# A gate's column sums: from dot products on VectorE to scaled rows added up in DRAM

## The chip, the core and the metric

The kernel runs on one core of one Trainium2 chip. The metric is the device time of one execution in microseconds (us), as the median over the runs. TensorE is called PE here, VectorE DVE, ScalarE ACT, GpSimd POOL; SP is the engine that issues most transfers.

## The reference, cut to what matters

The reference is one decoder block on 512 tokens of width 1024, with a conditioning vector `c`. All that the change touches hangs on the first line:

```
mod = silu(c) @ w_ada + b_ada                                  # 1024 x 6144
shift1, scale1, gate1, shift2, scale2, gate2 = split(mod, 6)
h = rms_norm(x, norm1_g) * (1.0 + scale1) + shift1
z = h @ w_in            # u, v (gMLP), q, k, v, indexer q, k, weights, branch gates g_a, g_b
...                     # gMLP gives y_a; sparse attention (indexer, top 256 keys, softmax) gives y_b
merged = sigmoid(g_a) * (y_a @ w_proj_a) + sigmoid(g_b) * (y_b @ w_proj_b)
x = x + gate1 * (merged @ w_out)
h2 = rms_norm(x, norm2_g) * (1.0 + scale2) + shift2
x = x + gate2 * ((silu(f_g) * f_u) @ w_ffn_out)                # f_g, f_u = split(h2 @ w_ffn_in)
```

`mod` is a product of a vector with a matrix of 24 MB: six sections of 1024 outputs, each a sum over 1024 channels. In the attention, each query keeps the 256 best keys by an indexer score, which here means 16 rounds of "take the eight largest, strike them out" for a block of 128 queries with enough keys.

## The kernel before, in words

**The matrix products.** PE works in float32 by three products of rounded parts: every weight chunk is split into a rounded part `hi` (ACT, line 167) and a remainder `lo` (DVE or POOL, line 171), and each product is hi*hi + hi*lo + lo*hi (`mm3`, lines 105 to 109). A chunk is 128 x 1024 elements, 512 KB.

**The stream.** The weights come in one list `stream`, written by hand in the order of use. Between the weight chunks stand the rows of `w_ada` ("m" entries). `get(i)` returns chunk `i` and first calls `ensure`, which splits all chunks up to two ahead and does the work of every row that lies between; `room` says how many loads may be under way. Weight chunks share a ring of three `raw` tiles. Rows have tiles of their own (`mraw`) up to the end of the branch projections, use the `raw` ring in the stretch of the branch gates `W_GB`, and other tiles after that.

**The rows.** For section `s` and outputs 128*kt to 128*kt + 127, `mod_row(s, kt)` loads a tile of 128 outputs by 1024 channels and forms 128 dot products with silu(c), which stands in all partitions of `csb`. It does so in one of two ways: by one DVE instruction that multiplies and sums (line 270), or, with `pool=True`, by a product on POOL (line 266) and a summing copy on ACT (line 267). The latter is deferred through `part_sum` and `flush_rows`, by two calls of `get`. Section 4 is gate1, 2 and 3 are shift2 and scale2. The generator `mods_mid` gives the rows their order: eight of gate1, eight of section 2 (from the third on with POOL), eight of section 3. Gate1 is needed along the free axis; so after its last row `gate_out` turns it (a transpose on DVE, four writes to DRAM) and `gate_in` reads it back into all partitions, both called from a list of due times (`sec_done`, counted by `tick`).

**The order around the change.** After the gMLP products come eight groups, two weight chunks each: ga(0), ga(1), pa(0), pa(1), ga(2), pa(2), ga(3), pa(3), so 16 chunk steps, 0 to 15 (`au_tasks`, line 1280). In each step DVE is given some of the top-k work: `run_bg` takes from a list as much as a budget in us says (`BG`, line 1272, with 3.9 for steps that it doesn't name). In steps 12 and 13, after that, the first queries are split (`at_split`, line 1297). In steps 14 and 15 attention starts, and from then on `at_step(s)` (line 1482) runs the attention units, a block of 128 queries and two heads each, in a pipeline: scores on PE (`at_qk`), mask and maximum on DVE (`at_soft_a`), exponential on ACT (`at_exp`), normalisation on DVE (`at_soft_b`), turning, and the product with the values (`at_pv`). The first four units are turned through DRAM: DVE transposes (`at_turn`), SP writes (`at_out`), POOL reads back (`at_in`, tile `ld`), and `at_halves` splits. Between them, `gb_part` gives PE pieces of the branch gate B (tiles `pgb`, copied by ACT to `gb`, line 1477). Steps 2 to 7 take up to 2 us of top-k each (line 1514), and `need_sco` (line 893) forces what is left when a unit needs its mask: units 0 to 3 the mask of query block 3, units 4 to 7 block 2, units 8 to 11 block 1.

**Queues.** Each engine does its instructions in the order in which the code emits them, and an instruction that waits holds up all behind it. SP issues the loads; POOL issues the adding transfers and the reads of `ld`.

Of the kernel before, what the change touches and what calls it, by code (L numbers as in the profile page):

```python
# [58 lines left out]
def block_kernel(ctx: ExitStack, tc: tile.TileContext, x, x_t, w_in,  # L59
# [67 lines left out]
    def issue(i):  # L127
        e = stream[i]
        if e["kind"] == "m" and e["early"]:
            k = mrot[0]  # L130
            mrot[0] += 1
            raw = s2pair(k % 8, F32).rearrange("p a n -> p (a n)")
        elif i in last_raw:
            raw = last_raw[i]()
        elif e["kind"] == "m" and e["mid"]:
            k = e["mid"]
            if k == "A2":
                k = ("G1", "A2")[mrot[1] % 2]
                mrot[1] += 1
            raw = mid.tile([128, 1024], F32, name="mraw", tag=k, bufs=1)  # L140
        else:
            raw = base.tile([128, 1024], F32, name="raw", tag="raw", bufs=RAWB)
        e["raw"] = raw
        if e["kind"] == "m":
            e["dma"](raw)
            return
        k0, nk, n = e["kts"][0], len(e["kts"]), e["n"]
        e["view"] = lambda t: t[:, :nk * n].rearrange("p (j n) -> p j n", j=nk)
        SY.dma_start(raw[:, :nk * n], e["src"](k0, nk, e["c0"] if isinstance(e["c0"], tuple) else ((e["c0"], n),)))
        if i in W1[2:7]:  # L150
            load_xt(W1.index(i) + 1)
# [37 lines left out]
    def room(i):  # L189
        e = stream[i]  # L190
        if i in last_raw:
            return True
        pend = [stream[k] for k in range(st["prep"], i) if k not in last_raw]
        if e["kind"] == "m" and e["early"]:
            return sum(p["kind"] == "m" for p in pend) < 8
        if e["kind"] == "m" and e["mid"]:
            return all(p["kind"] == "w" for p in pend) and len(pend) <= 1
        return sum(p["kind"] == "w" or not (p["early"] or p["mid"]) for p in pend) + len(part_sum) < RAWB


    def get(i, ahead=2):
        k = wseq.index(i)
        asked[0] += 1
        flush_rows(2)
        ensure(wseq[min(k + ahead, len(wseq) - 1)])
        return chunk[i]

# [9 lines left out]
    mid = mid_stack.enter_context(tc.tile_pool(name="mid", bufs=1))  # L217
    csb = base.tile([128, D], F32, name="csb", tag="csb", bufs=1)
    crow = mid.tile([128, D], F32, name="crow", tag="A0", bufs=1)[0:1]
    pack = mid.tile([128, 211], F32, name="pack", tag="A2", bufs=1)  # L220
    SY.dma_start(pack, small)
    A.dma_start(crow, c_row)
    vmid = mid_stack.enter_context(tc.tile_pool(name="vmid", bufs=1))
# [15 lines left out]
    dram = ctx.enter_context(tc.tile_pool(name="dram", bufs=1, space=bass.MemoryType.DRAM))  # L239
    grow = [dram.tile([1, D], F32, name=f"grow{g}") for g in range(2)]  # L240

    part_sum, asked = [], [0]

    def flush_rows(age):
        while part_sum and part_sum[0][0] + age <= asked[0]:
            part_sum.pop(0)[1]()

    def mod_row(s, kt, pool=False):
        k = slice(kt, kt + 1)
        if s < 4:  # L250
            o = G1[:, s, k] if s < 2 else Gc[:, 1, 8 * (3 - s) + kt:8 * (3 - s) + kt + 1]
        else:
            o = gcol[:, 8 * (s - 4) + kt:8 * (s - 4) + kt + 1]
        scale, init = ((1.0, bsh1), (n1c[:, k], bsc1), (1.0, bsh2), (n2c[:, k], bsc2), (1.0, bg1), (1.0, bg2))[s]

        whole = s > 1 or kt
        parts = [slice(0, D)] if whole else [slice(0, 512), slice(512, D)]
        sums = [init[:, k], o] if whole else [init[:, k], half_sum[:, s:s + 1], o]

        def dma(raw):  # L260
            for c in list(parts):
                SY.dma_start(raw[:, c], w_shsc[s * D + kt * 128:s * D + (kt + 1) * 128, c])

        def fn(raw, n=2):
            if pool:
                P.tensor_mul(raw, raw, csb)
                part_sum.append((asked[0], lambda: A.activation(raw, raw, AF.Copy, scale=scale, accum_out=o)))
                return
            for c in [parts.pop(0) for _ in range(min(n, len(parts)))]:
                V.tensor_tensor_reduce(out=raw[:, c], in0=raw[:, c], in1=(csb if s > 1 else pc)[:, c], scale=scale,  # L270
                                       scalar=sums.pop(0), op0=OP.mult, op1=OP.add, accum_out=sums[0])
        return dma, fn

    def gate_out(g):
        V.transpose(gturn, gcol)
        rows = grow[g].rearrange("o (k b j) -> (o k) b j", b=4, j=32)
        for b in range(4):
            SY.dma_start(rows[:, b], gturn[32 * b + 8 * g:32 * b + 8 * g + 8])

    def gate_in(g):  # L280
        SY.dma_start(gate_b[1 + g], grow[g][0].partition_broadcast(128))

    def gate1_row(kt):
        dma, dot = mod_row(4, kt)

        def fn(raw):
            dot(raw)
            if kt == 7:
                sec_done.append((tick[0] + 2, lambda: gate_out(0)))
                sec_done.append((tick[0] + 5, lambda: gate_in(0)))  # L290
        return dma, fn

    def group(src, c0, n=256, K=8, mods=None, pool=False, where=None, nm=1, mraw="A2"):
        ids = []
# [18 lines left out]
    W_Q += [group(w_in, 2048 + 256 * g) for g in range(2, 4)]  # L313

    def mods_mid():
        for kt in range(8):
            yield gate1_row(kt)
        for s in (2, 3):
            for kt in range(8):
                yield mod_row(s, kt, s == 2 and kt > 1)  # L320
    mm_ = mods_mid()
    W_GA, W_PA = {}, {}
    for kind, g in (("a", 0), ("a", 1), ("p", 0), ("p", 1), ("a", 2), ("p", 2), ("a", 3), ("p", 3)):
        if kind == "a":
            W_GA[g] = group(w_in, 4168 + 256 * g, pool=2 * (g > 1), mods=mm_ if g > 1 else None)
        else:
            W_PA[g] = group(w_pa, 256 * g, pool=2, mods=mm_ if g < 3 else None)
    W_GB = [group(w_in, 5192 + 256 * g, pool=2 * (g == 1), mods=mm_ if g else None, mraw=False) for g in range(4)]
    for i in W_GB[1]:
        stream[i]["lo"] = V  # L330
# [96 lines left out]
    V.tensor_copy(cols[:, 0:67], pack[:, 0:67])  # L427
    posi = pack[:, 67:195].bitcast(I32)
    P.tensor_copy(half_sum[:, 16:32], pack[:, 195:211])
    lng, lnb, wrow = half_sum[:, 16:24], half_sum[:, 24:32], gcol[:, 16:24]  # L430

    ones = mid.tile([128, 128], F32, name="ones", tag="A3", bufs=1)
# [836 lines left out]
    austep = [0, 0]  # L1269
    MM = {0: [3, 4], 1: [5, 6], 2: [7]}  # L1270
    EV = {0: [1, 2], 1: [3, 4], 2: [5, 6], 3: [7]}
    BG = {0: 0.0, 1: 0.0, 2: 0.0, 3: 1.0, 4: 1.8, 5: 2.5, 7: 2.5, 8: 1.8, 11: 2.5, 12: 3.0, 13: 3.0, 14: 1.0, 15: 1.0}
    PT = {4: [pq0.turn], 5: [pq0.put], 6: [pq0.scatter, pq4.fetch], 8: [pq4.turn], 9: [pq4.put], 10: [pq4.scatter]}

    def au_post():
# [4 lines left out]
    def au_tasks():  # L1280
        s = austep[0]
        austep[0] += 1
        if s == 0:
            k_b(1)
        for m in EV.get(s, []):
            mix_ev(m)
        for fn in PT.get(s, []):
            fn()
        run_bg(BG.get(s, 3.9))
        if s in (12, 13):  # L1290
            at_split(s - 12)

    aun = [(i, hp) for i in (3, 2, 1, 0) for hp in range(4)]
    AS = {}
# [252 lines left out]
    for s in range(2, NU + 3):  # L1547
        at_step(s)

    flush_rows(0)  # L1550
    V.tensor_add(Gc[:, 1, 10:16], Gc[:, 1, 10:16], bsh2[:, 2:8])
    for g in range(4):
        A.activation(gbt[g], gbt[g], AF.Sigmoid)
    for i in range(4):
# [796 lines left out]
```

## Time and profile before

| | |
|---|---|
| median of the 3 runs | 809.16 us (807.22 to 810.09) |
| the profiled execution's own time | 807.56 us |
| its span | 805.8 us |
| mean granted clock of TensorE | 0.985 |
| instructions | 13081 |
| row loads of `w_ada` into `mraw`, into `raw` | 26 of 512 KB, 6 of 512 KB |

The span runs from the first to the last instruction of the profiled execution; 1.8 us lie around it. In the timeline a line holds the start in us, the duration in us, engine, line of the kernel, operation, result <- operands, shapes and count; the bracket at its end is the idle time of that engine ahead of it and what ended it. In the tables of stretches each engine's column is its busy time in us, with the number of instructions behind it.

### The profile page before, as it was taken

How to read it: one execution, taken by the hardware profiler on the slowest of the kernel's cores; microseconds unless marked ns; L12 is line 12 of the kernel's file. 1: busy time of each engine (PE TensorE's matmuls, PEld its weight loads, DVE VectorE, ACT ScalarE, POOL GpSimd, SP SyncE). 2: the span in 40 equal slices, each digit the busy share in tenths (PEclk: the TensorE clock that was granted, in tenths of full speed). 3: DMA queues.
4: the chain of work that ended last, by engine and by line, in shares of the span. 5: the costliest groups of instructions: out<-in, count | busy, mean ns of one | idle time of the engine just before them, and what ended most of it. 6: DMA issues, size and time to landing. Idle time of an engine off the chain costs nothing.

```text
span 805.8 us, 13081 instructions
## 1 busy us (share of the span) xinstructions
PE 778.0 (97%) x4867; PEld 701.7 (87%) x4867; DVE 692.7 (86%) x1115; ACT 464.1 (58%) x829; POOL 192.0 (24%) x266
## 2 busy tenths in 40 slices
PE   8999999999999998799999999999999999999996
PEld 6899899999888786678887789999999999888885
DVE  7979778878899989987669888989999888898886
ACT  6665567575512356456625577556565656766654
POOL 5981323220244214312020010312122222100001
PEclk9999999999999998999999999999999999999999
DMA  9965777784476467227692612689987977566672
GB/s 356 414 183 165 172 177 198 192 239 142 131 235 198 143 165 203 79 74 236 238 274 66 204 58 79 176 256 290 259 287 201 281 197 210 162 193 197 217 226 108
DMA packets 56610, 158.71 MB, mean 197 GB/s; under 512 B 15873, under 2 KB 16513, under 8 KB 56546
## 3 DMA queue, kind: packets, MB, share of 16 engines
q1 hardware_dynamic: 43152, 118.49, 43.7%
q0 software_dynamic: 12816, 38.43, 20.4%
q8 instruction: 38, 0.62, 0.3%
q10 hardware_dynamic: 578, 0.95, 0.3%
q14 instruction: 26, 0.21, 0.1%
HBM read 151.53 MB, written 28.72 MB: 224 GB/s over the span
## 4 chain that ended last, share of the span: by engine, by line
PE 66%; DVE 19%; ACT 5%; DMA 4%; issue 4%; POOL 1%; SPq 0%; POOLq 0%; DVEq 0%; ACTq 0%
PE R L107 8%; PE R L109 8%; PE R L108 8%; PE pfo L109 4%; PE pfo L108 4%; PE pfo L107 4%; PE pav L107 3%; PE pav L108 3%; PE pav L109 3%; DVE mraw L270 3%; DMA mraw<-in_w_shsc_dram 2%; DVE sco L874 2%; PE pb L107 2%; PE pb L109 2%; PE pb L108 2%
## 5 line engine op out<-in xcount | busy, mean ns | idle before, releaser
L167 ACT ACTIVATE hi<-raw 128x1024 fp32r<-128x1024 f32 (+4 forms) x90 | 90.4, 1007 | 80.3 <-PE pfo L109 22.6
L171 DVE TENSOR_TENSOR lo<-raw,hi 128x1024 fp32r<-128x1024 f32 (+3 forms) x70 | 84.6, 1209 | 23.3 <-ACT hi L167 23.2
L108 PE MATMUL pfo<-lo,za 128*128 128x512 f32 (+1 forms) x144 | 55.2, 383 | 0.0
L109 PE MATMUL pfo<-hi,za 128*128 128x512 f32 (+1 forms) x144 | 55.2, 383 | 0.0
L107 PE MATMUL pfo<-hi,za 128*128 128x512 f32 (+1 forms) x144 | 55.2, 383 | 0.0
L401 POOL COPY sm<-sm 128x1 f32<-128x1 f32 x36 | 24.0, 666 | 103.4 <-ACT sm L400 103.3
L107 PE MATMUL pb<-h,hi 128*128 128x512 f32 (+1 forms) x128 | 48.5, 379 | 0.0
L109 PE MATMUL pb<-h,lo 128*128 128x512 f32 (+1 forms) x128 | 48.1, 376 | 0.0
L108 PE MATMUL pb<-h,hi 128*128 128x512 f32 (+1 forms) x128 | 48.1, 376 | 0.0
L270 DVE CUSTOM_DVE_ANT_0 mraw<-mraw,csb,cols 128x1024 f32<-128x1024 f32 x26 | 38.2, 1471 | 7.2 <-DMA mraw<-in_w_shsc_dram 7.2
L171 POOL TENSOR_TENSOR lo<-raw,hi 128x1024 fp32r<-128x1024 f32 x12 | 29.1, 2428 | 63.6 <-ACT hi L167 63.6
L107 PE MATMUL R<-tb,sx 128*128 128x256 f32 x160 | 44.2, 276 | 0.0
L109 PE MATMUL R<-tb,sx 128*128 128x256 f32 x160 | 44.2, 276 | 0.0
L108 PE MATMUL R<-tb,sx 128*128 128x256 f32 x160 | 44.2, 276 | 0.0
L107 PE MATMUL R<-tb,hi 128*128 128x256 f32 x160 | 44.2, 276 | 0.0
L108 PE MATMUL R<-tb,hi 128*128 128x256 f32 x160 | 44.2, 276 | 0.0
L109 PE MATMUL R<-tb,lo 128*128 128x256 f32 x160 | 44.2, 276 | 0.0
L381 POOL DMA_DIRECT2D wsum<-in_w_ffn_out_dram x24 | 19.6, 831 | 62.5 <-DMA wsum<-wsum 35.4
L108 PEld LDWEIGHTS pfo<-lo,za 128*128 128x128 f32 x144 | 27.1, 188 | 5.4
L107 PEld LDWEIGHTS pfo<-hi,za 128*128 128x128 f32 x144 | 27.1, 188 | 5.3
L109 PEld LDWEIGHTS pfo<-hi,za 128*128 128x128 f32 x144 | 27.1, 188 | 5.3
L107 PE MATMUL pgb<-h,hi 128*128 128x512 f32 x64 | 27.8, 434 | 3.9 <-ACT gb L1477 3.9
(438 smaller groups left out, 2908.4 us busy)
## 6 DMA issues: line engine op xcount, KB each, us to landing
raw<-in_w_ffn_in_dram SPq DMA_DIRECT2D x44, 512.0 KB, 5.6
raw<-in_w_in_dram SPq DMA_DIRECT2D x36, 512.0 KB, 3.6
wsum<-in_w_ffn_out_dram POOLq DMA_DIRECT2D x30, 512.0 KB, 7.3
mraw<-in_w_shsc_dram SPq DMA_DIRECT2D x26, 512.0 KB, 4.1
raw<-wsum SPq DMA_DIRECT2D x20, 512.0 KB, 4.1
s<-in_w_shsc_dram SPq DMA_DIRECT2D x14, 512.0 KB, 8.1
raw<-in_w_ffn_out_dram SPq DMA_DIRECT2D x13, 512.0 KB, 3.9
wsum<-wsum POOLq DMA_DIRECT2D x10, 512.0 KB, 5.7
```

Source lines behind the costliest of these rows:

```text
L107: T.matmul(o, wh, rh, start=start, stop=False, **kw)
L108: T.matmul(o, wh, rlo, start=False, stop=False, **kw)
L109: T.matmul(o, wlo, rh, start=False, stop=stop, **kw)
L167: A.activation(hi[:, :m], e["raw"][:, :m], AF.Copy)
L171: e["lo"].tensor_sub(lo[:, :m], e["raw"][:, :m], f(hi[:, :m]))
L270: V.tensor_tensor_reduce(out=raw[:, c], in0=raw[:, c], in1=(csb if s > 1 else pc)[:, c], scale=scale, scalar=sums.pop(0), op0=OP.mult, op1 ...
L381: P.dma_start(wsum_at(n, c), src, max_dma_last_dim=4096, accum_op=OP.add)
L401: P.tensor_copy(t, t)
L874: V.match_replace(out=sco[i], in_to_replace=m8s[i], in_values=sco[i], imm_value=TAKEN)
```

## The change

Gate1 is no longer formed by dot products. Its part of `w_ada` is handed over untransposed, so that a row tile holds 128 channels by 1024 outputs. ACT scales each tile by silu(c) of its channels (one factor for each partition, `ccol`); POOL writes the first scaled tile to `gacc` in DRAM and adds the other seven to it by adding transfers. What is left to sum are the 128 partitions: two adding transfers within DRAM fold 128 rows to 64 and to 32, four loads bring these into SBUF in blocks of 32 by 32, DVE transposes and sums them and adds the bias. Then `gate_out` and `gate_in` go on as before, at later due times.

The rows of section 2 are all done by DVE; the products on POOL, their sums on ACT and the later addition of the bias are gone. The rows of gate1 begin two groups earlier and are spread thinner, one for each group at first, with two rows of section 2 among the last of them; they go round three tiles in place of two. The top-k budgets are raised in steps 4 to 10, 12, 14 and 15, and cut in 11 and 13; the default is 4.6. In steps 12 and 13 the queries are split ahead of the top-k work.

```diff
-                k = ("G1", "A2")[mrot[1] % 2]
+                k = ("G1", "A2", "L")[mrot[1] % 3]
...
-        return sum(p["kind"] == "w" or not (p["early"] or p["mid"]) for p in pend) + len(part_sum) < RAWB
+        return sum(p["kind"] == "w" or not (p["early"] or p["mid"]) for p in pend) < RAWB
...
-        flush_rows(2)
+        flush_rows(1)
...
-            if pool:
-                P.tensor_mul(raw, raw, csb)
-                part_sum.append((asked[0], lambda: A.activation(raw, raw, AF.Copy, scale=scale, accum_out=o)))
-                return
...
+    gacc = dram.tile([128, D], F32, name="gacc")
+
     def gate1_row(kt):
-        dma, dot = mod_row(4, kt)
+
+        def dma(raw):
+            SY.dma_start(raw, w_shsc[4 * D + kt * 128:4 * D + (kt + 1) * 128])
+
+        def add(raw):
+            if kt:
+                P.dma_start(gacc, raw, accum_op=OP.add)
+            else:
+                P.dma_start(gacc, raw)
+            if kt == 7:
+                t0 = tick[0]
+                for k, fn in ((2, lambda: gate_fold(64)), (4, lambda: gate_fold(32)), (6, gate_load), (8, gate_sum),
+                              (8, lambda: gate_out(0)), (11, lambda: gate_in(0))):
+                    sec_done.append((t0 + k, fn))
 
         def fn(raw):
-            dot(raw)
-            if kt == 7:
-                sec_done.append((tick[0] + 2, lambda: gate_out(0)))
-                sec_done.append((tick[0] + 5, lambda: gate_in(0)))
+            A.activation(raw, raw, AF.Copy, scale=ccol[:, kt:kt + 1])
+            part_sum.append((asked[0], lambda: add(raw)))
         return dma, fn
+
+    def gate_fold(n):
+        P.dma_start(gacc[:n], gacc[n:2 * n], max_dma_last_dim=4096, accum_op=OP.add)
+
+    def gate_load():
+        gt.append(base.tile([128, 8, 32], F32, name="gt", tag="acc", bufs=2))
+        for q in range(4):
+            SY.dma_start(gt[0][32 * q:32 * q + 32], gacc[:32].rearrange("i (k q j) -> q i k j", q=4, j=32)[q])
+
+    def gate_sum():
+        t = base.tile([128, 8, 32], F32, name="gt", tag="acc", bufs=2)
+        V.transpose(t.rearrange("p k j -> p (k j)"), gt[0].rearrange("p k j -> p (k j)"))
+        V.tensor_reduce(gcol[:, 0:8], t, op=OP.add, axis=AX.X)
+        V.tensor_add(gcol[:, 0:8], gcol[:, 0:8], bg1)
...
     def mods_mid():
-        for kt in range(8):
-            yield gate1_row(kt)
-        for s in (2, 3):
-            for kt in range(8):
-                yield mod_row(s, kt, s == 2 and kt > 1)
+        for k in (0, 1, 2, 3, 4, 5, -1, 6, -2, 7):
+            yield gate1_row(k) if k >= 0 else mod_row(2, -1 - k)
+        for s, k0 in ((2, 2), (3, 0)):
+            for kt in range(k0, 8):
+                yield mod_row(s, kt)
...
-            W_GA[g] = group(w_in, 4168 + 256 * g, pool=2 * (g > 1), mods=mm_ if g > 1 else None)
+            W_GA[g] = group(w_in, 4168 + 256 * g, pool=2 * (g > 1), mods=mm_, nm=(1, int(g == 3)))
         else:
-            W_PA[g] = group(w_pa, 256 * g, pool=2, mods=mm_ if g < 3 else None)
+            W_PA[g] = group(w_pa, 256 * g, pool=2, mods=mm_, nm=(1, int(g == 2)))
...
+    ccol = cols[:, 67:75]
+    A.activation(ccol, pack[:, 211:219], AF.Silu)
...
-    BG = {0: 0.0, 1: 0.0, 2: 0.0, 3: 1.0, 4: 1.8, 5: 2.5, 7: 2.5, 8: 1.8, 11: 2.5, 12: 3.0, 13: 3.0, 14: 1.0, 15: 1.0}
+    BG = {0: 0.0, 1: 0.0, 2: 0.0, 3: 1.0, 4: 2.7, 5: 3.4, 7: 3.4, 8: 2.7, 11: 2.2, 12: 3.8, 13: 2.5, 14: 1.5, 15: 1.2}
...
-        run_bg(BG.get(s, 3.9))
         if s in (12, 13):
             at_split(s - 12)
+        run_bg(BG.get(s, 4.6))
...
-    flush_rows(0)
-    V.tensor_add(Gc[:, 1, 10:16], Gc[:, 1, 10:16], bsh2[:, 2:8])
```

More of the change, by code (lines that the diff above doesn't have):

```diff
@@ L137, in issue @@
             if k == "A2":
-                k = ("G1", "A2")[mrot[1] % 2]
+                k = ("G1", "A2", "L")[mrot[1] % 3]
                 mrot[1] += 1
-            raw = mid.tile([128, 1024], F32, name="mraw", tag=k, bufs=1)
+            raw = (vmid if k == "L" else mid).tile([128, 1024], F32, name="mraw", tag=k, bufs=1)
         else:
@@ L219, in block_kernel @@
     crow = mid.tile([128, D], F32, name="crow", tag="A0", bufs=1)[0:1]
-    pack = mid.tile([128, 211], F32, name="pack", tag="A2", bufs=1)
+    pack = mid.tile([128, 219], F32, name="pack", tag="A2", bufs=1)
     SY.dma_start(pack, small)
@@ L240, in block_kernel @@
     grow = [dram.tile([1, D], F32, name=f"grow{g}") for g in range(2)]
-    part_sum, asked = [], [0]
+    part_sum, asked, gt = [], [0], []
     def flush_rows(age):
@@ L246, in flush_rows, with mod_row @@
             part_sum.pop(0)[1]()
-    def mod_row(s, kt, pool=False):
+    def mod_row(s, kt):
         k = slice(kt, kt + 1)
@@ L2328 @@
          _np.repeat(_np.asarray(inputs["positions"]).reshape(4, 1, 128), 32, axis=1).reshape(128, 128).view(_np.float32),
-         col(inputs["gmlp_ln_g"]), col(inputs["gmlp_ln_b"])],
+         col(inputs["gmlp_ln_g"]), col(inputs["gmlp_ln_b"]), col(inputs["c"])],
         axis=1)
@@ L2335 @@
     w_ada = _np.asarray(inputs["w_ada"])[0]
-    given["w_shsc"] = _np.concatenate([w_ada[:, k * 1024:(k + 1) * 1024] for k in (0, 1, 3, 4, 2, 5)], axis=1).T
+    given["w_shsc"] = _np.concatenate(
+        [w_ada[:, k * 1024:(k + 1) * 1024] if k == 2 else w_ada[:, k * 1024:(k + 1) * 1024].T for k in (0, 1, 3, 4, 2, 5)])
     for name in _plan():
```

## The prediction

> **What bounds the kernel now.** I read the page first, for the shares of the engines and the chain that ended last, then a table of stretches around the edited code (with the granted clock), then the timeline of each engine there, and the waits of SP's queue last.
>
> ```profile
> PE 778.0 (97%) x4867; PEld 701.7 (87%) x4867; DVE 692.7 (86%) x1115; ACT 464.1 (58%) x829; POOL 192.0 (24%) x266
> PE 66%; DVE 19%; ACT 5%; DMA 4%; issue 4%; POOL 1%; SPq 0%; POOLq 0%; DVEq 0%; ACTq 0%
> 219.70:279.80 60.10, 58.25 (x257) 47.88 (x257) 58.79 (x110) 15.37 (x20) 25.67 (x11) 1.00 0.61 193
> 279.80:291.90 12.10, 12.10 (x48) 9.74 (x47) 8.73 (x22) 7.32 (x14) 0.00 (x0) 0.86 0.22 62
> 291.90:347.80 55.90, 46.06 (x223) 39.09 (x222) 54.25 (x127) 28.38 (x64) 19.94 (x21) 0.88 0.55 156
> 347.80:394.00 46.20, 45.03 (x252) 38.60 (x251) 32.27 (x102) 33.13 (x78) 4.52 (x5) 1.00 0.56 194
> ```
>
> The last four rows are stretches: length, then busy time of PE, weight loads, DVE, ACT and POOL, granted clock, DMA share, GB/s. Over the whole span TensorE is the bound, 778.0 of 805.8 us. Not so in one stretch: from 291.9 to 347.8, attention steps 2 to 7, PE is busy 46.06 of 55.9 us while DVE is busy 54.25. There DVE sets the pace, and the clock falls to 0.88. Before it (219.7 to 279.8) both are full, PE 58.25 and DVE 58.79 of 60.1; after it PE is the bound again (45.03 of 46.2) and DVE has 14 us free. So a microsecond of DVE is worth a microsecond in attention steps 2 to 7, and almost nothing in the two stretches beside them. PE's timeline shows where it stood:
>
> ```profile
> 278.44 0.50 PE L109 MATMUL qk<-k_hi,ql 128*128 128x512 f32 x1 [1.85 <-DVE ql L1308]
> 279.95 0.61 PE L109 MATMUL pb<-y,lo 128*128 128x512 f32 x1
> 283.34 0.41 PE L108 MATMUL pb<-y,hi 128*128 128x512 f32 x1
> ...
> 311.53 0.79 PE L107 MATMUL pgb<-h,hi 128*128 128x512 f32 x1 [3.92 <-ACT gb L1477]
> 317.46 0.31 PE L107 MATMUL pv<-th,v_hi 128*128 128x256 f32 x1
> 331.65 1.57 PE L1431 MATMUL pT<-ident,pt 128*128 128x128 f32 x6 [2.88 <-DVE pt L1391]
> 343.58 0.35 PE L107 MATMUL pv<-th,v_hi 128*128 128x256 f32 x1 [1.63 <-DVE yb L1460]
> ```
>
> The bracket is PE's idle time and what ended it. After each wait the matmuls are slow for some microseconds: from 279.95 to 283.34 eight pass, 0.42 us apart, where from 278.44 to 279.95 six passed, 0.25 apart.
>
> **The change, part by part.**
>
> *The queries' split goes ahead of the top-k work (steps 12 and 13).*
>
> ```profile
> 275.01 0.54 DVE L874 MATCH_REPLACE8 sco<-m,sco 128x384 f32<-128x384 f32 x1
> 277.98 0.42 DVE L1308 TENSOR_TENSOR ql<-qf,qh 128x256 fp32r<-128x256 f32 x1
> ```
>
> The second ql stood behind top-k instructions from 275.01 to 277.98, and PE waited 1.85 us for it. Put ahead, it is ready about 3 us earlier and the wait goes. The slow matmuls behind it go too: (283.34 - 279.95) - 8 x 0.25 = 1.4 us. That is 3.3 us, on PE, which was full up to there and is again after. The 0.86 of that stretch is the granted clock behind these rows. [...]
>
> *Gate rows off DVE.* Eight products of line 270 leave the stretch from 219.7 on.
>
> ```profile
> 219.70:279.80 60.10, 17.37 (x20) 1.00 0.61 193
> 253.12 1.28 DVE L270 CUSTOM_DVE_ANT_0 mraw<-mraw,csb,cols 128x1024 f32<-128x1024 f32 x1
> 254.32 0.42 DVE L877 TENSOR_SCALAR sco<-sco 128x512 f32<-128x512 f32 x1
> 309.87 1.04 ACT L267 ACTIVATE raw<-raw 128x1024 f32<-128x1024 f32 x1
> ```
>
> The first row is line 270 alone in that stretch: 10 products (20 records) in 17.37 us. An undisturbed one takes 1.20 from its start to the next instruction; two of the ten stay, so 17.37 - 2 x 1.28 = 14.8 us leave. In comes top-k: the budgets that the code gives it in these steps (BG, in us) add up to 31.8 before and 38.2 after, so 6.4 us. The net is -8.4; or -3.8 if the 4.6 us by which the eight exceed 8 x 1.28 were stalls beside GpSimd that some other instruction will now meet. Either way DVE gets lighter here and nothing of it is on PE's path, apart from the ql above. ACT takes the eight scalings at 1.04 each, 8.3 us on an engine that is busy 15.4 of 60.1; I cost them at nothing, and 8.3 if that cover were gone. The order of ACT: a scaling waits for its row, and the next weight's hi is behind it; that hi is wanted two chunks later.
>
> *Eight adding transfers on POOL.*
>
> ```profile
> L1024 POOL DMA_DIRECT2D avr<-in_w_in_dram x8: 869/984/1243, 82.6 to 177.7; - x8
> DMA to landing us min/median/max: 5.3/7.5/10.4
> 237.67 2.41 POOL L171 TENSOR_TENSOR lo<-raw,hi 128x1024 fp32r<-128x1024 f32 x1 [2.76 <-ACT hi L167]
> 243.11 2.40 POOL L171 TENSOR_TENSOR lo<-raw,hi 128x1024 fp32r<-128x1024 f32 x1 [3.03 <-ACT hi L167]
> ```
>
> No transfer that adds into DRAM from SBUF stands in this stretch. The nearest, an add of 512 KB from DRAM into SBUF, takes 0.98 us to issue and lands after 5.3 to 10.4. A weight chunk passes every 5.44 us (237.67 to 243.11) and POOL idles 2.8 to 3.0 us of it. An add is issued one chunk after its scaling, so it finds its data ready; adds follow each other by one group of two chunks, 10.9 us, longer than the longest landing, so the wait for the previous sum is over too. Behind it on POOL stands the next lo, whose reader is PE two chunks on. Cost: nothing, with 0.98 inside 2.8 idle us; from both sides, zero to the rival below. As DMA time the adds put some 8 x 512 KB on a stretch that is at 0.61. The three row tiles and the earlier, thinner spread of rows are what keeps the adds apart; no cost.
>
> *No GpSimd products in attention.* This and the next part carry the gain.
>
> ```profile
> 303.90 2.41 POOL L266 TENSOR_TENSOR raw<-raw,csb 128x1024 f32<-128x1024 f32 x1
> 304.88 2.52 DVE L171 TENSOR_TENSOR lo<-raw,hi 128x1024 fp32r<-128x1024 f32 x1
> 312.94 1.23 DVE L171 TENSOR_TENSOR lo<-raw,hi 128x1024 fp32r<-128x1024 f32 x1
> 317.68 2.40 POOL L266 TENSOR_TENSOR raw<-raw,csb 128x1024 f32<-128x1024 f32 x1
> 317.29 3.08 DVE L1307 TENSOR_TENSOR ql<-qf,qh 128x256 fp32r<-128x256 f32 x1
> 331.76 0.41 DVE L1307 TENSOR_TENSOR ql<-qf,qh 128x256 fp32r<-128x256 f32 x1
> 326.58 4.70 POOL L266 TENSOR_TENSOR raw<-raw,csb 128x1024 f32<-128x1024 f32 x2
> 326.45 5.39 DVE L1391 TENSOR_SCALAR pt<-pt,mx 128x384 f32<-128x384 f32 x2
> 339.65 0.75 DVE L1391 TENSOR_SCALAR pt<-pt,mx 128x384 f32<-128x384 f32 x2
> ```
>
> Each product is paired with the DVE instruction that overlaps it and the same instruction alone: 2.52 against 1.23, 3.08 against 0.41, 5.39 against 0.75. DVE stood still for 1.3 + 2.7 + 4.6 = 8.6 us. That goes. Instead DVE does the six rows itself, at 1.20: in the order of the code the stream asks for three of them in steps 3, 4 and 6 (POOL ran ahead of that order) and three after 347.8, where DVE has 14 us free. So +3.6 on the path. ACT loses its six sums of 1.04; one stood directly ahead of the gb copy for which PE waited 3.92 us.
>
> *Top-k no longer ends there.*
>
> ```profile
> 332.09 0.41 DVE L871 MAX8 m<-sco 128x8 f32<-128x256 f32 x1
> 334.39 0.41 DVE L1460 TENSOR_TENSOR yb<-pv,yb 128x256 fp32r<-128x256 f32 x1
> 340.66 0.08 DVE L874 MATCH_VALUE_LOAD sco<-m,sco 128x8 f32 x1
> 343.02 0.41 DVE L1460 TENSOR_TENSOR yb<-pv,yb 128x256 fp32r<-128x256 f32 x1
> 344.89 0.42 DVE L871 MAX8 m<-sco 128x8 f32<-128x256 f32 x1
> 347.80 0.43 DVE L1366 CUSTOM_DVE_ANT_0 pt<-qk,sco 128x256 f32<-128x256 f32 x1
> ```
>
> Three runs of top-k, each from its first instruction to the one after it: 2.3, 2.4 and 2.9 us, the last of them forced because step 8 needs the mask. By the code's own costs the whole top-k is 55.3 us, of which 9.1 come before the BG steps; so 14.4 are left over for attention, and 8.0 after the change, which steps 2 to 5 use up at 2.0 each. So these 7.6 us go.
>
> *The fold and the column sums.* Two folds on POOL, four loads and the writes of the gate on SP, and a transpose, a reduction and an addition of at most 128x256 on DVE. On DVE I take the 128x256 price above, 0.41, twice, and 0.2 for the small ones: +1.0, in step 6. On POOL each fold follows the loads of `ld` of its step and has a whole step until the next; on SP there is room, since its weight loads are waiting for buffers (35.1 us below), not for the queue.
>
> ```profile
> SPq L149 <- DVE lo L171: 35.1, 5, 14.5
> ```
>
> Sum for attention steps 2 to 7 on DVE: -8.6 + 3.6 - 7.6 + 1.0 = -11.6 of 55.9. Does PE then bind? PE's 46.06 hold slow matmuls: from 311.53 to 317.46 fifteen take 5.9 us where 15 x 0.25 = 3.8 would do, and behind each of the waits at 331.65 and 343.58 I put the 1.4 found above (an estimate): 46.06 - 2.1 - 2.8 = 41.2 at full clock. DVE's 55.9 - 11.6 = 44.3 stays above that, so the 11.6 can go. With the 3.3 ahead of it: 14.9. I take off 3 for hand-overs between engines that are no longer hidden once DVE is not saturated, an estimate from the 1.85, 1.63 and 2.88 us waits above, one of which I expect to stay. Forecast -12, from the profiled execution's 807.56 us to 795.6. That execution lies 1.6 below the median of the runs shown (809.16), so the median after is 809.16 - 12 = **797.2**.
>
> **Rivals.**
>
> *Less is handed over (0.16).* DVE's order is fixed, and with the waits for ACT and PE showing up in it, only the first 3.3 us and about a fourth of the 11.6 (2.9) reach the end: 6.2 less, 803.0. For it: from 279.8 to 291.9 DVE is busy only 8.73 of 12.1 us although attention has begun. Against it: 54.25 of 55.9 us busy is work, not waiting.
>
> *Given back later (0.08).* The attention stretch gets shorter, but the branch projection after it waits for its weights and rows, whose transfers begin when attention's buffers come free. Then all but about a microsecond returns: 808. For it: DMA shares of 0.56 and more after 347.8. Against it: the loads are released by the same instructions, which also come earlier.
>
> *POOL in its own queue: slower (0.10).* [...] The rival decides from the point where an add lands later than 10.9 us: POOL then stands at the next add with a lo behind it. The lo, done 1.0 + 2.4 us into a chunk and wanted 10.9 us after its start, has 7.5 us of slack, so PE waits from landings of about 18 us on. At 20 us, 2 us for each of the 7 dependent adds and about 3 for each fold, which would hold back the `ld` loads: 14 + 6 = 20, less the 12: 817. Against it: 10.4 us is the longest landing of the nearest rows.
>
> **How the numbers follow.** The forecast has 0.66, and its own range is 791 to 801.7: at the far end attention steps 2 to 7 shrink to PE's 41.2 (14.7, and 3.3 ahead of it: -18), at the near end half of 14.9 is lost. I extend it to 805.5 to take in the first rival, which leaves out the other two: 0.18. A measurement of this kernel can tell about 0.3% (2.4 us) from no change. Faster by more than that: 0.66 + 0.16 = 0.82. Within it: 0.08. Slower: 0.10.
>
> **What would show it.** Right: no POOL tensor instruction after about 275; the stretch from the first softmax to step 8 (55.9 us) at 43 to 46; lo, ql and pt at 1.23, 0.41 and 0.75 throughout; no top-k after step 5; PE idle there under 4 us and the clock near 1.0; no wait of qk for ql. Wrong: POOL idle before an add with a DMA named as releaser and PE waiting for lo between 219 and 280; new DVE waits for ACT of the size of what was removed; or a longer stretch after step 8.

## The result, and the profile after

| | before | after |
|---|---|---|
| median | 808.59 us (807.22 to 810.09, 4 runs) | 793.97 us (793.75 to 794.63, 4 runs) |
| the profiled execution | 807.56 us | 794.63 us |
| its span, granted clock | 805.8 us, 0.985 | 792.9 us, 0.991 |

The ratio is 0.982 (95% interval 0.980 to 0.984): faster by 14.6 us, where 12 were forecast. The two profiled executions, one below and one above its kernel's median, differ by 12.9. The page of the kernel after, its busy times and the chain that ended last:

```profile
PE 771.6 (97%) x4867; PEld 698.4 (88%) x4867; DVE 681.1 (86%) x1113; ACT 466.5 (59%) x826; POOL 187.0 (24%) x270
PE 77%; DVE 11%; ACT 4%; DMA 4%; issue 3%; POOL 0%; POOLq 0%; DVEq 0%; SPq 0%; ACTq 0%
```

And its table of stretches, cut at the same events as before (the first softmax, the start of step 2, the softmax of step 8; columns as in the prediction):

```profile
219.70:278.90 59.20, 59.20 (x263) 48.98 (x261) 55.94 (x112) 21.44 (x26) 31.25 (x17) 1.00 0.78 214
278.90:290.70 11.80, 11.80 (x53) 9.74 (x52) 8.95 (x23) 6.17 (x13) 0.60 (x1) 1.00 0.64 143
290.70:335.90 45.20, 37.78 (x201) 32.80 (x201) 43.54 (x116) 24.80 (x58) 9.56 (x18) 0.92 0.75 196
```

DVE's share of the chain fell from 19% to 11%. Attention steps 2 to 7 take 45.20 us in place of 55.9. The first softmax comes 0.86 us earlier (278.90 for 279.76), the softmax of step 8 then 11.9 (335.90 for 347.80), and the last 1.0 of the 12.9 us by which the span fell comes later. In steps 2 to 7 DVE is still busy nearly all the time, 43.54 of 45.20; its busy time fell by 10.7, as much as the stretch. Its timeline there, in four groups: lo, ql and pt, which GpSimd had held up; the rows that DVE took over; the end of top-k; the gate's column sums:

```profile
305.60 1.22 DVE L171 TENSOR_TENSOR lo<-raw,hi 128x1024 fp32r<-128x1024 f32 x1
317.91 0.42 DVE L1332 TENSOR_TENSOR ql<-qf,qh 128x256 fp32r<-128x256 f32 x1
324.21 0.75 DVE L1416 TENSOR_SCALAR pt<-pt,mx 128x384 f32<-128x384 f32 x2
...
304.40 1.27 DVE L266 CUSTOM_DVE_ANT_0 raw<-raw,csb,cols 128x1024 f32<-128x1024 f32 x1
311.83 1.28 DVE L266 CUSTOM_DVE_ANT_0 raw<-raw,csb,cols 128x1024 f32<-128x1024 f32 x1
325.55 1.27 DVE L266 CUSTOM_DVE_ANT_0 raw<-raw,csb,cols 128x1024 f32<-128x1024 f32 x1
...
320.20 0.29 DVE L902 TENSOR_SCALAR sco<-sco 128x256 f32<-128x256 f32 x1
...
327.89 0.43 DVE L312 STREAM_TRANSPOSE gt<-gt 128x256 f32<-128x256 f32 x1
328.36 0.42 DVE L313 TENSOR_REDUCE gcol<-gt 128x8 f32<-128x256 f32 x1
```

1.22, 0.42 and 0.75 stand where 2.52, 3.08 and 5.39 stood; three rows fall in these steps, as counted; top-k ends in step 5. Two things were not forecast. PE's wait for the gb copy grew from 3.92 to 6.13 us, and ACT waits for gate rows ahead of attention, which delays DVE there:

```profile
309.92 0.79 PE L107 MATMUL pgb<-h,hi 128*128 128x512 f32 x1 [6.13 <-ACT gb L1502]
261.22 1.16 ACT L298 ACTIVATE mraw<-mraw,cols 128x1024 f32<-128x1024 f32 x1 [6.69 <-DMA mraw<-in_w_shsc_dram]
274.12 1.15 ACT L298 ACTIVATE mraw<-mraw,cols 128x1024 f32<-128x1024 f32 x1 [9.07 <-DMA mraw<-in_w_shsc_dram]
276.29 2.41 POOL L171 TENSOR_TENSOR lo<-raw,hi 128x1024 fp32r<-128x1024 f32 x1 [7.25 <-ACT hi L167]
277.08 0.72 ACT L1330 ACTIVATE qh<-qf 128x256 fp32r<-128x256 f32 x2
277.52 1.46 DVE L1333 TENSOR_TENSOR ql<-qf,qh 128x256 fp32r<-128x256 f32 x1 [1.34 <-ACT qh L1330]
```

The scaling at 274.12 holds back the hi and the qh that stand behind it on ACT. DVE waits 1.34 us for qh, and the ql that follows stands beside POOL's late lo and takes 1.46 us in place of 0.42. The first softmax stands directly behind that ql. Without the late row it could start 1.4 to 2.4 us earlier (an estimate: PE's last score ends at 277.46, and the two delays are 1.34 + 1.04).

### The profile page after: what moved, and what is told of

The parts are those of the page before. It is cut to its first block, busy times and chain, and to the rows that moved or that the text cites. A ratio compares the mean times of both kernels' runs of the same rounds, so it can differ in the third digit from the quotient of the medians.

```text
span 792.9 us, 13095 instructions
## 1 busy us (share of the span) xinstructions
PE 771.6 (97%) x4867; PEld 698.4 (88%) x4867; DVE 681.1 (86%) x1113; ACT 466.5 (59%) x826; POOL 187.0 (24%) x270
## 4 chain that ended last, share of the span: by engine, by line
PE 77%; DVE 11%; ACT 4%; DMA 4%; issue 3%; POOL 0%; POOLq 0%; DVEq 0%; SPq 0%; ACTq 0%
PE R L108 8%; PE R L107 8%; PE R L109 8%; PE pb L108 5%; PE pb L109 5%; PE pb L107 5%; PE pfo L108 4%; PE pfo L109 4%; PE pfo L107 4%; PE pav L107 3%; PE pav L108 3%; PE pav L109 3%; DMA mraw<-in_w_shsc_dram 1%; PE pv L108 1%; DVE lo L171 1%
## 5 line engine op out<-in xcount | busy, mean ns | idle before, releaser
L171 DVE TENSOR_TENSOR lo<-raw,hi 128x1024 fp32r<-128x1024 f32 (+3 forms) x70 | 81.7, 1168 | 22.9 <-ACT hi L167 22.8
L424 POOL COPY sm<-sm 128x1 f32<-128x1 f32 x36 | 27.6, 765 | 91.3 <-ACT sm L423 91.3
L108 PEld LDWEIGHTS R<-tb,hi 128*128 128x128 f32 x160 | 30.0, 188 | 0.0
```

Of the source, the lines that this page charges most:

```text
L108: T.matmul(o, wh, rlo, start=False, stop=False, **kw)
L171: e["lo"].tensor_sub(lo[:, :m], e["raw"][:, :m], f(hi[:, :m]))
L424: P.tensor_copy(t, t)
```

## The experiments

The theory under test: DVE sets the pace in attention steps 2 to 7, a microsecond of its work there is one of the time (so far the prediction), and PE's gains ahead of it are waited away. Rival one, which the prediction's sum had in it: PE's own waits and slow stretches count, the split's 3.3 us above all. Rival two: the gain is the end of GpSimd's stalls and little else. Every ratio below is to the kernel before, on the same chip; the medians come from several chips, on which the kernel before took 807.3 to 808.6 us. "First" and "step 8" are the starts of those softmaxes on DVE in the profiled execution.

| kernel | median us | ratio (95%) | first | step 8 | span |
|---|---|---|---|---|---|
| before | 808.59 | 1 | 279.76 | 347.80 | 805.8 |
| split_only | 810.92 | 1.0039 (1.0022 to 1.0055) | 282.00 | 349.57 | 810.3 |
| rows_dve | 800.26 | 0.9914 (0.9895 to 0.9933) | 279.71 | 341.63 | 798.4 |
| gate_only | 807.43 | 0.9994 (0.9981 to 1.0007) | 278.13 | 347.90 | 804.9 |
| after | 793.97 | 0.982 (0.980 to 0.984) | 278.90 | 335.90 | 792.9 |
| old_budget | 800.61 | 0.9915 (0.9896 to 0.9934) | 278.49 | 343.01 | 798.7 |
| dot_gate | 796.13 | 0.9852 (0.9838 to 0.9866) | 281.49 | 336.74 | 794.3 |
| pool_rows | 802.70 | 0.9930 (0.9917 to 0.9942) | 278.21 | 341.35 | 798.8 |
| split_late | 794.52 | 0.9843 (0.9826 to 0.9861) | 279.79 | 336.30 | 793.8 |
| no_adds | 794.43 | 0.9833 (0.9817 to 0.9848) | 280.15 | 337.33 | 795.7 |
| early_rows | 793.25 | 0.9820 (0.9806 to 0.9835) | 278.45 | 335.36 | 791.3 |
| more_budget | 794.38 | 0.9832 (0.9811 to 0.9853) | 279.20 | 335.33 | 790.9 |
| shift_two | 793.03 | 0.9818 (0.9803 to 0.9832) | 279.81 | 335.72 | 791.2 |
| comb_one | 794.39 | 0.9840 (0.9826 to 0.9854) | 279.57 | 335.60 | 792.7 |

**split_only**: one part alone.

```diff
-        run_bg(BG.get(s, 3.9))
         if s in (12, 13):
             at_split(s - 12)
+        run_bg(BG.get(s, 3.9))
```

> The kernel before with one edit: the high/low split of a step's queries stands ahead of the top-k pieces in steps 12 and 13. The wait of qk for ql (1.85 us at 278.44) should go in every theory. If VectorE sets the pace of attention steps 2 to 7, the 3.3 us that TensorE gains are waited away a little later and the time falls by 0 to 1 us (808 to 809). If TensorE's own waits and half-rate stretches count one for one, it falls by 3.3 us (about 805.5).

It became slower by 3.1 us, which neither theory had, and PE's wait for ql did not go but fell to 1.04 us. PE and DVE around the first softmax, and POOL:

```profile
278.32 0.39 PE L109 MATMUL qk<-k_hi,ql 128*128 128x512 f32 x1
270.20 2.39 POOL L171 TENSOR_TENSOR lo<-raw,hi 128x1024 fp32r<-128x1024 f32 x1 [3.04 <-ACT hi L167]
270.22 2.65 DVE L1308 TENSOR_TENSOR ql<-qf,qh 128x256 fp32r<-128x256 f32 x1
282.00 0.68 DVE L1366 CUSTOM_DVE_ANT_0 pt<-qk,sco 128x512 f32<-128x512 f32 x1
```

And the same two places before:

```profile
279.25 0.40 PE L109 MATMUL qk<-k_hi,ql 128*128 128x512 f32 x1
279.76 0.68 DVE L1366 CUSTOM_DVE_ANT_0 pt<-qk,sco 128x512 f32<-128x512 f32 x1
```

PE finished the scores 0.93 us earlier and the softmax that reads them started 2.24 us later. DVE never waited in the 60 us ahead of its softmax; the ql that was put forward now stood beside POOL's lo and took 2.65 us in place of 0.41. Those 2.24 us are the delay to the hundredth. So DVE, not PE, sets the start of attention in this kernel, and rival one falls. (1.8 us of the delay are there at step 8; the rest of the 3.1 comes later, and its cause is open.)

**rows_dve**: GpSimd's products go to DVE, nothing else.

```diff
-                yield mod_row(s, kt, s == 2 and kt > 1)
+                yield mod_row(s, kt)
...
-    V.tensor_add(Gc[:, 1, 10:16], Gc[:, 1, 10:16], bsh2[:, 2:8])
```

> The kernel before with one edit: the six w_shsc rows that GpSimd multiplied in attention steps 3 to 7 are multiplied and summed by VectorE (1.2 us each, 7.2 us in all; the addition of their biases near the end goes). In the changed kernel only three such rows are left in these steps, so this is not that part alone. If the stalls that GpSimd's products put on VectorE (8.6 us) are what the change won, the time falls by 8.6 - 7.2 = 1.4 us with six rows on VectorE, up to 5 if two or three of the six come after step 7. If the two engines' sharing costs nothing, the time rises by 3 to 7 us.

6.9 us faster by the ratio, beyond the 5 that I gave it, although DVE does six more products, three of them before step 8. The first softmax did not move; between it and step 8 it gained 6.1 us, 5.6 of them in DVE's busy time (the third busy column). The kernel before, then this run:

```profile
279.76:347.80 68.04, 58.20 (x269) 48.88 (x268) 63.02 (x147) 35.74 (x78) 19.94 (x21) 0.88 0.49 140
279.71:341.63 61.92, 54.94 (x271) 46.24 (x269) 57.45 (x154) 32.70 (x72) 7.89 (x16) 0.94 0.54 153
```

**old_budget** and **more_budget**: the amount of top-k ahead of attention.

```diff
-    BG = {..., 4: 2.7, 5: 3.4, 7: 3.4, 8: 2.7, 11: 2.2, 12: 3.8, 13: 2.5, 14: 1.5, 15: 1.2}      # after; others 4.6
+    BG = {..., 4: 1.8, 5: 2.5, 7: 2.5, 8: 1.8, 11: 2.5, 12: 3.0, 13: 3.0, 14: 1.0, 15: 1.0}      # old_budget; others 3.9
+    BG = {..., 4: 3.1, 5: 3.8, 7: 3.8, 8: 3.1, 11: 2.6, 12: 4.2, 13: 2.9, 14: 1.5, 15: 1.2}      # more_budget; others 4.8
```

> The changed kernel with the budgets of top-k pieces per step of before, so that less of the top-k lies ahead of the attention and more in steps 4 to 8. If VectorE sets the pace there, each us of top-k handed back costs a us: 6 to 7.6 us more than the changed kernel (800 to 801.5). If GpSimd's stalls or the split were the gain, under 2 us more (794 to 796).

> The changed kernel with 0.2 to 0.4 us more of top-k pieces in each step from 4 on, some 2.8 us in all, taken out of attention steps 4 and 5. If VectorE sets the pace in attention and has room before it, up to 2.8 us less than the changed kernel (about 791.5). If VectorE is by now full ahead of attention (48.98 us busy of 59.2, TensorE 59.2 of 59.2), some of it comes back as waits of TensorE: the same or up to 2 us more.

old_budget lost 6.6 us by the medians, 7.7 by the ratios, and 7.5 between first softmax and step 8 (64.5 us in place of 57.0; 6.3 of the 7.5 are busy time of DVE). That is the theory's number, and rival two, which gave it under 2, falls. more_budget cannot be told from the changed kernel: the slope of one for one ends right there. What DVE waits for in step 4 of more_budget, and what that waits for:

```profile
313.31 1.06 ACT L167 ACTIVATE hi<-raw 128x1024 fp32r<-128x1024 f32 x1 [2.64 <-DMA raw<-in_w_in_dram]
314.40 1.23 DVE L171 TENSOR_TENSOR lo<-raw,hi 128x1024 fp32r<-128x1024 f32 x1 [2.60 <-ACT hi L167]
```

With the top-k gone from step 4, lo comes to wait for a weight load. After the change that same wait was 0.44 us. (The 48.98 us that the expectation gives as DVE's busy time is the column of the weight loads; DVE's is 55.94. The expectation of dot_gate has the same slip.)

**dot_gate**: the gate's products stay on DVE, with all the rest of the change; `w_shsc` is packed as before.

```diff
-            A.activation(raw, raw, AF.Copy, scale=ccol[:, kt:kt + 1])
-            part_sum.append((asked[0], lambda: add(raw)))
+            dot(raw)
+            if kt == 7:
+                sec_done.append((tick[0] + 2, lambda: gate_out(0)))
+                sec_done.append((tick[0] + 5, lambda: gate_in(0)))
```

> The changed kernel with the eight rows of the first gate multiplied and summed by VectorE again, as before, and no adding transfers and folds; the larger top-k budgets stay. VectorE gets back 14.8 us of dot products in the stretch ahead of attention and keeps its 6.4 us of earlier top-k: 8.4 us above what it had before there. If VectorE has the room (48.98 us busy of 59.2 with the rows away, so 63.8 of 59.2 with them), the time would be the changed kernel's; it has not by this sum, so TensorE should wait 4 to 6 us in that stretch, and the time be 798 to 801. If only GpSimd's stalls in attention mattered, the time is the changed kernel's, 794.

It lost 2.2 us (2.6 by the ratios), half of what I gave it; the two intervals still touch, so the loss is likely and not certain. PE did not wait before attention. Nor did 14.8 us of products come back: the rows begin two groups earlier now, and in this stretch line 266 takes 11.63 us in place of the changed kernel's 2.57. DVE is late instead, as its stretch ahead of attention and its first softmax show:

```profile
219.70:278.90 59.20, 59.20 (x263) 48.97 (x262) 57.41 (x118) 16.39 (x21) 27.43 (x11) 1.00 0.58 178
```

```profile
281.49 0.69 DVE L1380 CUSTOM_DVE_ANT_0 pt<-qk,sco 128x512 f32<-128x512 f32 x1
```

PE is busy 59.20 of 59.20 all the same; the first softmax is 2.59 us later, and 0.84 of that is left at step 8. Of the rest, 1.0 us are the column sums of the changed kernel (0.43 + 0.42 + 0.17), which this one does not do.

**gate_only**: the new way of the gate alone, everything else as before (the edit is pool_rows, below, with the old budgets and the late split).

> The kernel before with the new way of the first gate alone (rows scaled by ScalarE, adding transfers, folds, three row tiles); GpSimd's products, the budgets of top-k pieces and the late split are those of before. The budgets set how much top-k lies ahead of attention, so the 14.8 us that VectorE is rid of are left idle there: the start of attention comes 0.5 to 1.5 us earlier, the stretch behind it is the same, and the time falls by 0 to 2 us (806 to 808). If VectorE's freed time counted by itself, it would fall by more than 5 us (under 803).

0.9994: nothing. Its first softmax comes 1.63 us earlier, and at step 8 it is as late as before (347.90 for 347.80). What takes the 1.63 back is mostly the gate itself: its column sums and its turning now stand on DVE in between, at 334.78, with 0.44 + 0.42 + 0.17 + 0.21 = 1.2 us. Without top-k to fill it, most of the freed DVE time is empty: 49.83 of 58.4 us busy in the stretch from 219.7 to its first softmax, PE 58.40.

```profile
219.70:278.10 58.40, 58.40 (x259) 48.33 (x258) 49.83 (x91) 20.64 (x26) 31.02 (x17) 1.00 0.78 216
```

**pool_rows**: GpSimd's products back, in the changed kernel (with their deferral and the later addition of the bias).

```diff
-                yield mod_row(s, kt)
+                yield mod_row(s, kt, s == 2)
...
+            if pool:
+                P.tensor_mul(raw, raw, csb)
+                late_sum.append((asked[0], lambda: A.activation(raw, raw, AF.Copy, scale=scale, accum_out=o)))
+                return
```

> The changed kernel with the w_shsc rows from step 3 on multiplied by GpSimd again and summed by ScalarE, as before. If GpSimd's products stall VectorE where VectorE sets the pace, the time rises by about 5 us (8.6 of stalls less 3.6 of VectorE's own row products; 799), and lo, ql and pt show durations of 2.5 to 5.4 us again. If they cost nothing, it falls by 3.6 us (790.4).

8.7 us slower than the changed kernel by the medians, more than the 5 given (the profiled execution, the fastest of its kernel, is 5.9 slower). Its POOL products and the DVE instructions beside them:

```profile
305.34 2.36 POOL L271 TENSOR_TENSOR raw<-raw,csb 128x1024 f32<-128x1024 f32 x1
305.40 0.56 DVE L1400 CUSTOM_DVE_ANT_0 pt<-qk,sco 128x384 f32<-128x384 f32 x1
305.99 1.75 DVE L1402 TENSOR_SCALAR mx<-mx 128x2 f32<-128x2 f32 x1
325.50 4.70 POOL L271 TENSOR_TENSOR raw<-raw,csb 128x1024 f32<-128x1024 f32 x2
325.38 5.38 DVE L1425 TENSOR_SCALAR pt<-pt,mx 128x384 f32<-128x384 f32 x2
```

A scaling of two elements a lane, 0.17 us elsewhere, stood 1.75 us, until the product's end at 307.70. With ql (3.07 at 316.42) and pt (5.38) the stalls are 1.58 + 2.65 + 4.63 = 8.9 us; less three rows at 1.27, that is 5.1 of the 6.1 us by which the stretch from first softmax to step 8 is longer (63.1 for 57.0).

**split_late**: the old order of the split in the changed kernel.

> The changed kernel with the top-k pieces ahead of the split again in steps 12 and 13, as before. If the split's place sets TensorE's start into attention, qk waits for ql again (1.85 us and half-rate matmuls behind) and the time rises by 3.3 us (797.3). If VectorE sets the pace there, the sum of its work is the same in either order and the time stays within 1 us of 794.

0.6 us by the medians; the intervals overlap. The second ql's first reader does not wait, although top-k stands ahead of ql again; and as in the changed kernel, DVE's last ql ahead of the softmax waits for qh (1.40 us):

```profile
276.39 0.40 PE L109 MATMUL qk<-k_hi,ql 128*128 128x512 f32 x1
```

**no_adds** and **early_rows**: are the gate's transfers what ACT waits for, and does it matter?

```diff
-            if kt:
-                P.dma_start(gacc, raw, accum_op=OP.add)
-            else:
+            if not kt:                                                    # no_adds
                 P.dma_start(gacc, raw)
...
-            return all(p["kind"] == "w" for p in pend) and len(pend) <= 1
+            return all(p["kind"] == "w" for p in pend) and len(pend) <= 2   # early_rows
```

> The changed kernel without seven of the eight transfers of the gate's scaled rows (the first, which writes, and the folds stay, so the gate's sum holds 128 of 1024 channels only). If the adding transfers crowd out the row loads and weight loads, ScalarE's waits for rows fall under 3 us and the time falls by 1 to 2 us (792 to 793). If they cost nothing, as forecast, it stays at 794.

> The changed kernel with one edit: the gate's row loads may be issued with two transfers pending in place of one, so a chunk earlier. If ScalarE's waits for the rows (6.69 us at 261.22, 9.07 us at 274.12) delay the next hi and with it the first softmax of attention, these waits shrink under 3 us and the time falls by up to 2 us (792). If the transfers themselves are the limit (DMA share 0.93 to 1.01 from 230 to 260), the rows land no earlier and the time stays at 794, or other loads are late by as much.

Without the adds ACT's two waits fall from 6.69 and 9.07 us to 3.54 and 3.31: the adds do hold up the row loads. DVE no longer waits for qh either. Yet the time is the same, and the first softmax even 1.25 us later, because something else came in. On DVE a row product now stands beside a lo that POOL begins at another moment, and takes 3.19 us in place of 1.28; a scaling at 270.67 takes 2.57 in place of 0.36 in the same way:

```profile
258.17 1.15 ACT L296 ACTIVATE mraw<-mraw,cols 128x1024 f32<-128x1024 f32 x1 [3.54 <-DMA mraw<-in_w_shsc_dram]
268.45 1.16 ACT L296 ACTIVATE mraw<-mraw,cols 128x1024 f32<-128x1024 f32 x1 [3.31 <-DMA mraw<-in_w_shsc_dram]
260.35 2.41 POOL L171 TENSOR_TENSOR lo<-raw,hi 128x1024 fp32r<-128x1024 f32 x1 [3.25 <-ACT hi L167]
260.65 3.19 DVE L266 CUSTOM_DVE_ANT_0 mraw<-mraw,csb,cols 128x1024 f32<-128x1024 f32 x1
```

These two stalls are 4.1 us, more than the late row cost by the estimate above. So this run does not price the adds by themselves.

early_rows left the waits as they were (6.31 and 8.59) and the time too: this rule of `room` was not what delayed the loads.

**shift_two** and **comb_one**: attempts at a better version, from more_budget's wait.

```diff
-    W_GB = [group(w_in, 5192 + 256 * g, pool=2 * (g == 1), mods=mm_ if g else None, mraw=False) for g in range(4)]
+    W_GB = [group(w_in, 5192 + 256 * g, pool=2 * (g == 1), mods=mm_, nm=(1, 0, 1, 1)[g], mraw=False) for g in range(4)]
```

That is shift_two; comb_one has `nm=((1, 0), (1, 0), 1, 1)[g]` and the edits of early_rows and more_budget.

> The changed kernel with the two w_shsc rows of attention steps 3 and 4 multiplied two half-groups earlier, in steps 1 and 2, where VectorE waits 2.10 and 0.49 us for hi. If VectorE's work and the weight loads that share the queues with the rows (ScalarE's 2.12 us wait for a weight load at 312.47) set the pace of steps 3 to 5, the time falls by 1 to 2.5 us (792). If steps 1 and 2 are as tight, or the rows' loads come late there, it stays at 794 or rises by up to 2.5.

> The changed kernel with three edits together: the gate's row loads with two transfers pending (early_rows), the larger top-k budgets (more_budget), and one w_shsc row moved from step 3 to 4 ahead into steps 0 to 2. Alone the first two gave nothing that can be told from the changed kernel; more_budget was held up by a 2.60 us wait of lo for hi, which waits for a weight load behind a row load. With that row load out of the way the budgets' 2.8 us should count: 790 to 792. If another load takes its place, 793 to 794.

Neither can be told from the changed kernel. In shift_two the first softmax is 0.9 us later and steps 0 to 7 take 1.1 us less (55.9 for 57.0). In comb_one the wait for hi in step 4 shrank from 2.60 to 1.05 us, and a wait for ACT's copy of yb came up a step later:

```profile
312.63 1.23 DVE L171 TENSOR_TENSOR lo<-raw,hi 128x1024 fp32r<-128x1024 f32 x1 [1.05 <-ACT hi L167]
319.03 0.43 DVE L1485 TENSOR_TENSOR yb<-pv,yb 128x256 fp32r<-128x256 f32 x1 [1.63 <-ACT yb L1484]
```

No version was found that beats the changed kernel.

## Why the prediction was right, and where it was not

The sign, the place and the size were right: 10.7 us went in the stretch of steps 2 to 7, where the sum had 11.6. (The signs named there give the 55.9 us as beginning at the first softmax; they begin at step 2.) The terms, one by one:

*The base: DVE sets the pace in steps 2 to 7.* Right. old_budget puts top-k back and pays for it one for one; rows_dve and pool_rows move the time by DVE's stalls, and in steps 2 to 7 DVE's busy time and the stretch fell by the same 10.7 us. The rule has an end, which more_budget shows: beyond this change, DVE waits for hi (2.60 us in step 4).

*The split, 3.3 us.* Wrong, and the largest error. The step that failed is "That is 3.3 us, on PE, which was full up to there and is again after": I took PE's wait as a loss of time because PE was full on both sides. But the next thing that attention needs is a softmax, on DVE, and DVE was full as well, without a gap up to 279.76. split_only shows the two apart: PE earlier by 0.93, softmax later by 2.24. In the changed kernel the split's place is worth 0.6 us by the medians, not to be told from nothing. The wait itself did go in the changed kernel, and the slow matmuls are gone too (clock 1.00 in place of 0.86 in the second stretch). That such a wait brings them, for which 1.4 us of the 3.3 stand, holds for that execution only: in rows_dve PE waits the same 1.85 us at the same place and goes on at full clock (lines at the end). PE's lead was then given back at the gb copy, where its wait grew from 3.92 to 6.13 us.

*The gate off DVE, nothing on the path.* The sum is right, gate_only is 0.9994, but not its parts. DVE gains 1.63 us at the first softmax and gives them back for the column sums; and ACT's scalings, costed at nothing, hold up qh when a row is late, by 1.4 to 2.4 us at the first softmax of the changed kernel (the estimate above). Besides, the term is the room for the next but one: dot_gate, with the budgets and without the room, loses 2.2 us, likely and not certain. One way through the runs adds up: before 1, rows_dve 0.9914, dot_gate 0.9852, after 0.982. So the rows are worth some 7 us; the budgets, the split and the new order of the rows together some 5; and the gate's new way, the largest part of the diff, the last 2.6 (0.0032 of 808), which is near the noise.

*The adds, nothing.* Right on POOL. They took 0.87 us to issue and landed after 5.1 to 8.6 us. They were not 10.9 us apart but 7.1 (221.96 to 229.09) to 17.2, and each had landed before the next was issued; the slower rival never came near:

```profile
L288 POOL DMA_DIRECT2D gacc<-mraw x7: 843/868/952, 204.8 to 278.6; - x7
DMA to landing us min/median/max: 5.1/8.0/8.6
```

That POOL stands at an add until the transfer before it has landed, from which the rival's 817 is worked out, is seen once in the changed kernel: ahead of the first add its queue stood 6.79 us from 191.3 on, until the first write, issued at 191.31, had landed after 6.7; the other five such waits of line 288 took 0.02 us each. Whether the adds could overlap without it no run shows. What I had overlooked is the row loads beside them, which came late enough for ACT to wait 16 us in all. What that costs in the time stays open: no_adds, which shortens these waits, brings other stalls in.

*No GpSimd products, -8.6 + 3.6 = -5.0.* Right in the mechanism, too small. By itself it is worth 6.1 us between first softmax and step 8 and 6.9 in all. The stalls were sized well: between these events they come to 8.6 us in the kernel before and, counted in the same way, to 8.3 in split_only and 8.9 in gate_only and in pool_rows, beside some 9.5 us of products each time. The three rows were sized well too, at 3.8. Of the 1.1 us that the term lacks, half is a scaling of sco on DVE (0.81 us at 346.85, and 0.29 in rows_dve) and the other half shorter gaps of DVE; why they shrink is open. The DVE instruction that was held up ended after the POOL product beside it in each case shown: lo 1.1 us, ql 0.3 and pt 0.6 after it in the kernel before, and in pool_rows even a scaling of two elements 0.04 after it. Which instruction it was changed from run to run, as split_only (ql, 2.65 us) and no_adds (a row product, 3.19, and a scaling, 2.57) found out by accident beside POOL's lo; the sum hardly did. What decides it no run shows. The number of inputs alone does not: ql (2.65 us for 0.41 in split_only) has two tensors as input, pt (5.38 for 0.75) and mx (1.75 for 0.17) have one. And some were spared: the softmax's product, one of whose inputs is the matmul's result, took 0.56 us while a POOL product ran (pool_rows, 305.40) and 0.55 without one (the changed kernel, 307.28), and the two instructions of top-k, with one input, keep their durations beside a POOL lo of the changed kernel (0.54 and 0.56 without one, at 252.87 and 252.19):

```profile
254.62 2.40 POOL L171 TENSOR_TENSOR lo<-raw,hi 128x1024 fp32r<-128x1024 f32 x1 [2.91 <-ACT hi L167]
255.37 0.54 DVE L899 MATCH_REPLACE8 sco<-m,sco 128x384 f32<-128x384 f32 x1
255.95 0.56 DVE L896 MAX8 m<-sco 128x8 f32<-128x384 f32 x1
```

*Top-k out of steps 6 to 8, -7.6.* Right: 7.5 us between the same events in old_budget, where top-k ends only at 342.57, directly ahead of the softmax that needs it. Of these, 6.3 us are DVE's busy time, close to the 6.4 by which the budgets differ.

```profile
342.57 0.29 DVE L902 TENSOR_SCALAR sco<-sco 128x256 f32<-128x256 f32 x1
343.01 0.42 DVE L1391 CUSTOM_DVE_ANT_0 pt<-qk,sco 128x256 f32<-128x256 f32 x1
```

*The fold and the sums, +1.0.* 0.43 + 0.42 + 0.17 + 0.21 = 1.2 us, in step 6.

*Hand-overs, 3 us taken off.* The step that failed beside the split: of DVE's work in steps 2 to 7 10.7 us went, of the 11.6 in the sum, and all of it was handed over. PE's side of this was wrong: it idled 7.4 us in these steps, not under 4, at a clock of 0.92, and still did not hold DVE up. So 3.3 that did not come and 3 that were not lost cancelled, and by this luck the forecast came out near. The 0.86 at the first softmax, 0.3 in steps 0 and 1 and the last 1.0 us of the span were in no term. The rivals that forecast 803, 808 and 817 had each a place where they would have shown: the stretch of steps 2 to 7, the part after step 8 and POOL's adds. None showed there.

## What to carry to other kernels

Before an engine's wait is priced, ask which engine the next event needs, and look whether that one had a gap: a wait of a full engine (PE's 1.85 us) was worth nothing here, because the consumer behind it was full too. A large edit that frees an engine is worth only what another edit puts into the room (gate_only came to 0.9994), so time the filling apart from the freeing. Before work is put on an idle engine, look at what stands behind it there: the gate rows were free for ACT and still held up qh, for which DVE waited 1.34 us. And where two engines get in each other's way, price the time that the one occupies: the victims changed from run to run, their sum (8.3 to 8.9 us beside 9.5 us of products) hardly did.

## What the runs showed of the hardware that was not expected

- In pool_rows a DVE scaling of 128x2 elements beside a POOL product of 128x1024 took 1.75 us in place of 0.17, and ended as the product did (307.74 and 307.70).
- PE's clock: after the wait of 1.85 us in the kernel before, six matmuls went on at full speed and then eight came 0.42 us apart, at a clock of 0.50. In rows_dve the same wait at the same place was followed by none such, 0.23 us apart, and neither was 1.04 us in split_only. So the length of one wait does not settle whether the clock falls; what does is not shown. After 6.13 us in the changed kernel the mean clock of the step was 0.62 (second fence, the row of its stretch). In rows_dve:

```profile
278.39 0.50 PE L109 MATMUL qk<-k_hi,ql 128*128 128x512 f32 x1 [1.85 <-DVE ql L1308]
...
281.01 0.39 PE L108 MATMUL pb<-y,hi 128*128 128x512 f32 x1
281.23 0.39 PE L109 MATMUL pb<-y,lo 128*128 128x512 f32 x1
```

```profile
306.80:315.90 9.10, 5.98 (x20) 5.24 (x20) 8.43 (x21) 5.70 (x12) 0.00 (x0) 0.62 0.98 280
```

- An adding transfer of 512 KB from SBUF into DRAM landed after 5.1 to 8.6 us; with seven of them among row and weight loads, ACT's longest wait for a row load was 9.07 us, and without them 3.31 at the same place.
